# Hybrid recurrent decoder step: where the pre-sums of the last pairs are made in the down projection, when its forms are asked for, and where two loads and fillers stand in the mixer

## The chip, the cores and the metric

The kernel runs on 1 core of a Trainium2 chip. The metric is the time of one launch on the device, in microseconds (us). In the profile PE is TensorE (matmul), PEld its weight loads, DVE is VectorE, ACT is ScalarE, POOL is GpSimd, and SP is SyncE, whose queue issues all DMA transfers here.

## The reference, cut to what matters

One layer over 1024 prompt tokens and 8 x 4 sample tokens (1056 columns), D = 1024, FF = 2816, all in float32:

```
x = x + 0.5 * swiglu(rmsnorm(x, g1), w1_gu, w1_down)
x = x + Mix(rmsnorm(x, gm))            # mLSTM | retention | RG-LRU heads, then @ w_out
x = x + 0.5 * swiglu(rmsnorm(x, g2), w2_gu, w2_down)
y = rmsnorm(x, gf)

swiglu(x, w_gu, w_down):  gate, up = split(x @ w_gu);  (silu(gate) * up) @ w_down
```

Beside y the kernel returns the new recurrent states of both token sets.

## The kernel before, in words

Data lie transposed: a tile xT[k] holds 128 channels of all 1056 tokens. Every float32 operand is split into a high and a low float32r part, and every product takes three matmuls (low x high, high x low, high x high) of 264 columns in the two feed-forward parts.

**Feed-forward.** Each of the two feed-forward parts has a stage `gate_up` (gate and up projections) and a stage `down7` (down projection), and both use a seven-product scheme for 2 x 2 blocks: seven block products in place of eight, of sums and differences of blocks ("forms"). `gate_up` (line 474) runs over the 22 tiles j of FF. For each j, `gu` does its matmuls and stores the tile h(j) to DRAM (`hd`, lines 471 and 472). When both tiles of a pair p = j // 2 are there, `h_forms(p)` (line 490) is written behind the next j: it loads the two tiles back (`hr`, line 495), makes four sums on DVE (`ta`, `tb`), splits seven forms into high and low on ACT and DVE, and stores each form to DRAM (`hf`, line 507): 2 loads, 11 DVE operations, 7 ACT operations and 7 stores a pair. The pairs 0 to 7 of the ten (NP7 = 10, LATE7 = 2) are treated so. Pairs 8 and 9 wait for `down7`.

`down7` (line 545) takes the pairs in five groups of two; below they are the first to the fifth group, `gi` = 0 to 4. In each group it runs over four blocks of output channels (`mp` = 0 to 3), each with weights of its own (`down_weights`, line 522: one load of `wr`, sums on DVE, splits on ACT and DVE into `wh` and `wl`) and seven products of 12 matmuls, whose results DVE adds into xT (`add`, line 560). The 14 forms of a group stay on chip for its four blocks. After block 0 of a group the forms of the next group are asked for (line 588: 13 of them there, the fourteenth after the group, line 594). In the first group the order was another one: `h_forms(8)` after block 0, `h_forms(9)` after block 1, and the next group's forms after block 2.

**Slots.** All these wide tiles (xT, forms, hr, ta, tb) come from one pool, `blk`, of 35 slots. In `gate_up` 28 of them hold the forms of the normalised x, half of which are last read by the last j with both halves (19), the other half by j = 21. In `down7` 8 hold xT, 14 the forms of the group at work, and 13 are left for the next group's forms or for `h_forms`.

**Order of the work.** A scheduler orders each engine's instructions when the program is built, by their place in the program and by priority; the order is then fixed, and each engine runs its own list in order and waits at each instruction for what it needs. `tc.high_priority(n)` moves instructions up by n places: 100 for the loads of forms, 200 for weights, 300 for the additions that free PSUM.

**Mixer.** Near its end the mLSTM loop (`mlstm_loop`, line 1043) runs nine chunks of tokens with small matmuls and long chains on DVE, ACT and POOL. Between the chunks `fill(n)` (line 1518) puts n pieces of the output projection `w_out_main` (line 1505), 18 matmuls of 264 columns each, two pieces a unit m. xT was parked in DRAM before; its tiles 0 to 3 come back ahead of the loop, and tile m of 4 to 7 is asked for at unit m (line 1508). After the loop three pieces stand ahead of `norm` (line 1171), which normalises the heads in three column chunks c: scalings on ACT and DVE, then transposes on PE.

Of the kernel before, what the change touches and what calls it, by code (L numbers as in the profile page):

```python
# [24 lines left out]
KT = D // P  # L25
# [9 lines left out]
AHEAD = 100  # L35
AHEAD_GU = 200
AHEAD_EV = 300
LATE7 = 2
NP7 = 10
# [49 lines left out]
def build(ctx, tc, I, O, cdP, cd4):  # L89
# [19 lines left out]
    def B(name, dt=F32):  # L109
        return blk.tile([P, PITCH], dt, name=name, tag="b")[:, :BW]  # L110
# [79 lines left out]
    def split(h, l, x):  # L190
        act.copy(h, x)  # L191
        tt(l, x, h, SUB)
# [183 lines left out]
    def gu_weights(wgu, j):  # L376
        with tc.high_priority(AHEAD_GU):
            g = raw([wgu[:, j * P:(j + 1) * P]], KT, P)
            u = raw([wgu[:, FF + j * P:FF + (j + 1) * P]], KT, P)
            s12, s34 = wtile("wr", KT, P, F32), wtile("wr", KT, P, F32)  # L380
            lo, hi = slice(0, 4), slice(4, 8)
            tt(s12[:, lo], u[:, lo], u[:, hi], ADD)
            tt(s34[:, lo], g[:, lo], u[:, lo], ADD)
            tt(s12[:, hi], s12[:, lo], g[:, lo], ADD)
            tt(s34[:, hi], s12[:, hi], g[:, hi], ADD)
            hg, lg = parts(g)
            h12, l12 = parts(s12)
            h34, l34 = parts(s34)
            hu, lu = parts(u[:, hi])
        return [(hg[:, lo], lg[:, lo]), (hg[:, hi], lg[:, hi]), (h12[:, hi], l12[:, hi]), (h12[:, lo], l12[:, lo]),  # L390
                (h34[:, lo], l34[:, lo]), (h34[:, hi], l34[:, hi]), (hu, lu)]
# [82 lines left out]
    def gate_up(F, wgu, hd, hf, early, late, more):  # L474

        todo = [(j, [0, 1]) for j in range(FF // P) if j not in early + late]
        for i, j in enumerate(early):
            todo.insert(2 * i + 2, (j, [1]))
        todo += [(j, [1]) for j in late]
        ready, pend = set(), None  # L480
        for n, (j, ss) in enumerate(todo):
            gu(j, gu_weights(wgu, j), F, ss, hd, lambda: next(more, None))
            if pend is not None:
                h_forms(pend, hd, hf)
            ready.add(j)
            pend = j // 2 if j ^ 1 in ready and j // 2 < NP7 - LATE7 else None
        if pend is not None:
            h_forms(pend, hd, hf)

    def h_forms(p, hd, hf):  # L490

        v = lambda t: t.rearrange("p (s e n) -> p s e n", s=2, e=2)
        r = [B("hr") for _ in range(2)]
        for i in range(2):
            sp.dma_start(r[i], hd[(2 * p + i) * P:(2 * p + i + 1) * P, :])
        b11, b12, b21, b22 = (v(r[i])[:, :, e] for i in range(2) for e in range(2))
        w = lambda t: t.rearrange("p (i s n) -> p i s n", i=2, s=2)
        ta, tb = w(B("ta")), w(B("tb"))
        t1, t2, t3, t4 = ta[:, 0], ta[:, 1], tb[:, 0], tb[:, 1]
        tt(t1, b11, b12, SUB)  # L500
        stt(t2, t1, -1.0, b22, MUL, SUB)
        tt(t3, b22, b12, SUB)
        stt(t4, t2, -1.0, b21, MUL, SUB)
        for i, x in enumerate((b11, b21, t2, t1, t3, b22, t4)):
            f = B("hf", F32R)
            split(w(f)[:, 0], w(f)[:, 1], x)
            sp.dma_start(hf[p, i], f.bitcast(F32))
# [3 lines left out]
    ORDER = [0, 3, 2, 1, 4, 5, 6]  # L511

    def load_forms(ps_, hf, ii=ORDER):
        fs = [{} for _ in ps_]
        for i in ii:
            for d, p in zip(fs, ps_):
                f = B("hf", F32R)
                sp.dma_start(f.bitcast(F32), hf[p, i])
                d[i] = f.rearrange("p (i s n) -> p i s n", i=2, s=2)
        return fs  # L520
# [24 lines left out]
    def down7(xT, hd, hf, wd, first):  # L545
        groups = [(2 * i, 2 * i + 1) for i in range(NP7 // 2)]
        F = first

        def product(i, t, W, start):
            h, l = W[i]  # L550
            for s in range(2):
                o = t[:, s, :Q]
                for n, f in enumerate(F):
                    xh, xl = f[i][:, 0, s], f[i][:, 1, s]
                    st, sk = start and n == 0, not start
                    pe.matmul(o, l[:, n], xh, start=st, stop=False, skip_group_check=sk)  # L556
                    pe.matmul(o, h[:, n], xl, start=False, stop=False, skip_group_check=sk)  # L557
                    pe.matmul(o, h[:, n], xh, start=False, stop=n == len(F) - 1, skip_group_check=sk)  # L558

        def add(x, t, op=ADD):  # L560
            with tc.high_priority(AHEAD_EV):
                tt(x, x, t[:, :, :Q], op)

        for gi, g in enumerate(groups):
            nxt = []
            for mp in range(4):
                W = down_weights(wd, g, mp)
                x = [xT[2 * mp + i].rearrange("p (s e n) -> p s e n", s=2, e=2)[:, :, e] for i in range(2) for e in range(2)]
                x11, x12, x21, x22 = x
                b, c, a = (ps2(n) for n in ("db", "dc", "da"))  # L570
                product(0, b, W, True)
                with tc.high_priority(AHEAD_EV):
                    act.copy(a[:, :, :Q], b[:, :, :Q])
                product(3, c, W, True)
                add(x22, c, SUB)
                product(2, b, W, False)
                add(x12, b)
                product(1, a, W, False)
                add(x11, a)
                product(4, b, W, False)  # L580
                add(x22, b, SUB)
                product(5, c, W, False)
                add(x12, c)
                product(6, b, W, False)
                add(x21, b, SUB)
                if gi == 0 and mp < LATE7:
                    h_forms(NP7 - LATE7 + mp, hd, hf)
                if mp == (LATE7 if gi == 0 else 0) and gi + 1 < len(groups):
                    with tc.high_priority(AHEAD):
                        nxt = load_forms(groups[gi + 1], hf, ORDER[:6])  # L590
                        nxt[0].update(load_forms(groups[gi + 1][:1], hf, ORDER[6:])[0])
            if nxt:
                with tc.high_priority(AHEAD_GU):
                    nxt[1].update(load_forms(groups[gi + 1][1:], hf, ORDER[6:])[0])
            F = nxt
# [108 lines left out]
    def reload(ks=range(KT)):  # L704
        for k in ks:
            xT[k] = B(f"xT{k}")
            sp.dma_start(xT[k], spill[k * P:(k + 1) * P])
# [335 lines left out]
    def mlstm_loop(kT, qT, vtile, stile, ng, fc, ad, fill):  # L1043
# [127 lines left out]
        def norm():  # L1171
            mv2 = mv.rearrange("p (a c) -> p a c", c=2)
            rstd(rd, mv2[:, :, 1])
            stt(nmr, mv2[:, :, 0], -1.0, rd, MUL, MUL)
            for i in range(2):
                Y[i] = (B("yh", F32R), B("yl", F32R))
            for c, (c0, n) in enumerate(CH):
                for t in range(3 * c, 3 * c + 3):
                    for h in range(4):
                        hs = stile(t)[:, h * MD:(h + 1) * MD]  # L1180
                        a = 4 * t + h
                        if h % 2:
                            act.activation(hs, hs, AF.Identity, scale=rd[:, a:a + 1], bias=nmr[:, a:a + 1])
                        else:
                            tsc(hs, hs, rd[:, a:a + 1], MUL, nmr[:, a:a + 1], ADD)
                for i in range(2):
                    po = ps()
                    for j, o in tiles(c):
                        tr(po[:, o:o + P], stile(3 * c + j)[:, i * P:(i + 1) * P])
                    yh, yl = Y[i][0][:, c0:c0 + n], Y[i][1][:, c0:c0 + n]  # L1190
                    g = col("g_mlstm_norm", i)
                    act.mul(yh, po[:, :n], g)
                    stt(yl, po[:, :n], g, yh.bitcast(F32), MUL, SUB)
# [23 lines left out]
            if j == P8 + 1:  # L1217
                sample_update()
        statistics(NT - 1)
        fill(3)  # L1220
        norm()
        last_states()

# [281 lines left out]
    def w_out_main():  # L1505
        for s in range(2):
            for m in range(KT):
                if m > 3 and s == 0:
                    reload([m])
                u = unit([w_out[2 * P:, m * P:(m + 1) * P]], 6, P)  # L1510
                for q in (2 * s, 2 * s + 1):
                    w_out_part(ps("mm", "po"), u, 0, range(2, KT), 2, m, q)
                    yield
# [4 lines left out]
    def fill(n):  # L1518
        for _ in range(n):
            next(main, None)  # L1520
# [144 lines left out]
```

## Time and profile before

| | us |
|---|---|
| time, median of 3 runs | 2026.94 |
| the three runs | 2024.17, 2026.94, 2028.95 |
| the profiled execution, its own time | 2037.62 |
| its span, first to last instruction | 2035.8 |
| PE busy in the span | 1971.3 (97%) |
| DVE, ACT, POOL busy | 1379.8 (68%), 755.1 (37%), 128.0 (6%) |
| DMA moved | 347.03 MB, 170 GB/s on average |
| granted TensorE clock, mean | 0.982 |

The profile is of one execution, which took 10.68 us more than the median of the runs. A busy PE isn't PE at full speed: the granted clock stands beside it, as a share of full speed, and at half clock a matmul is busy for longer.

### The profile page before, as it was taken

To read this page: it belongs to the slowest core of one execution; us is meant where nothing else is said; L and a number is where in the kernel's file an instruction comes from. 1 tells how busy PE (TensorE), PEld (TensorE's weight loads), DVE (VectorE), ACT (ScalarE), POOL (GpSimd) and SP (SyncE) were. 2 spreads that over 40 slices of the span, in tenths; PEclk is the share of its full clock that TensorE was granted. 3 is DMA by queue.
4 is the path that set the end of the run, shared out by engine and by line. 5 is a ranking of instruction groups with operands and counts; after the bars stand their busy time and mean duration, and the time that the engine had idled before them with its cause. 6 is when DMAs were issued, how large, how long until landed. Compare 5 with 4: busy or idle time off the path is not lost.

```text
span 2035.8 us, 36906 instructions
## 1 busy us (share of the span) xinstructions
PE 1971.3 (97%) x15110; PEld 1932.2 (95%) x15110; DVE 1379.8 (68%) x2575; ACT 755.1 (37%) x1294; POOL 128.0 (6%) x175
## 2 busy tenths in 40 slices
PE   7999999999889999999999999999999999989998
PEld 7999999999889999999999989999999999978997
DVE  6857766647767775556668468976755664766777
ACT  6435444424222362211241324544434443422234
POOL 0000000000000033222111040000000000000000
PEclk9999999999989999999999989999999999989999
DMA  7236775667885432211111442425655566788522
GB/s 258 94 100 213 275 253 181 206 237 261 319 346 202 148 117 74 64 53 39 52 29 45 106 117 62 160 67 206 230 206 180 181 218 234 268 313 329 207 85 86
DMA packets 270927, 347.03 MB, mean 170 GB/s; under 512 B 17015, under 2 KB 219014, under 8 KB 270758
## 3 DMA queue, kind: packets, MB, share of 16 engines
q1 hardware_dynamic: 270758, 344.67, 49.1%
q8 instruction: 119, 1.95, 0.4%
q14 instruction: 50, 0.41, 0.1%
HBM read 224.82 MB, written 119.80 MB: 169 GB/s over the span
## 4 chain that ended last, share of the span: by engine, by line
PE 73%; issue 13%; DVE 7%; DMA 4%; ACT 2%; POOL 0%; SPq 0%; DVEq 0%; ACTq 0%; POOLq 0%
PE pb L430 8%; PE pb L431 7%; PE pb L432 7%; PE pj L199 4%; PE pj L200 4%; PE pj L201 4%; PE pc L431 4%; PE pc L430 4%; PE pc L432 4%; PE pa L431 2%; PE pa L430 2%; PE db L556 2%; PE pa L432 2%; PE db L557 2%; PE db L558 2%
## 5 line engine op out<-in xcount | busy, mean ns | idle before, releaser
L123 DVE TENSOR_TENSOR wl<-wr,wh 128x1024 fp32r<-128x1024 f32 (+3 forms) x442 | 362.4, 841 | 196.9 <-ACT wh L186 187.3
L186 ACT CAST wh<-wr 128x1024 fp32r<-128x1024 f32 (+2 forms) x242 | 230.0, 951 | 443.9 <-PE pj L201 146.1
L430 PE MATMUL pb<-fh,wl 128*128 128x264 f32 x1312 | 375.9, 287 | 5.3 <-DVE z L126 1.9
L431 PE MATMUL pb<-fl,wh 128*128 128x264 f32 x1312 | 373.0, 285 | 0.0
L432 PE MATMUL pb<-fh,wh 128*128 128x264 f32 x1312 | 370.4, 283 | 0.0
L430 PEld LDWEIGHTS pb<-fh,wl 128*128 128x128 f32 x1312 | 247.0, 188 | 10.2 <-DVE u L123 2.5
L431 PEld LDWEIGHTS pb<-fl,wh 128*128 128x128 f32 x1312 | 247.3, 188 | 0.0
L432 PEld LDWEIGHTS pb<-fh,wh 128*128 128x128 f32 x1312 | 247.1, 188 | 0.0
L556 PE MATMUL db<-hf,wl 128*128 128x264 f32 x640 | 187.4, 293 | 24.1 <-DVE wl L123 10.1
L123 DVE TENSOR_TENSOR wr<-wr 128x512 f32<-128x512 f32 (+1 forms) x336 | 176.1, 558 | 18.0 <-DMA wr<-in_w_ffn_gu 12.0
L199 PE MATMUL pj<-xh,wl 128*128 128x384 f32 (+1 forms) x576 | 187.8, 326 | 0.0
L201 PE MATMUL pj<-xh,wh 128*128 128x384 f32 (+1 forms) x576 | 187.0, 325 | 0.0
L557 PE MATMUL db<-hf,wh 128*128 128x264 f32 x640 | 185.8, 290 | 0.0
L200 PE MATMUL pj<-xl,wh 128*128 128x384 f32 (+1 forms) x576 | 185.8, 323 | 0.0
L558 PE MATMUL db<-hf,wh 128*128 128x264 f32 x640 | 184.9, 289 | 0.0
L430 PE MATMUL pc<-fh,wl 128*128 128x264 f32 x640 | 181.9, 284 | 0.0
L431 PE MATMUL pc<-fl,wh 128*128 128x264 f32 x640 | 181.8, 284 | 0.0
L432 PE MATMUL pc<-fh,wh 128*128 128x264 f32 x640 | 180.5, 282 | 0.0
L191 ACT CAST wh<-wr 128x256 fp32r<-128x256 f32 (+1 forms) x200 | 87.3, 490 | 246.8 <-PE dc L558 132.8
L556 PEld LDWEIGHTS db<-hf,wl 128*128 128x128 f32 x640 | 124.5, 195 | 27.6 <-issue 11.0
L558 PEld LDWEIGHTS db<-hf,wh 128*128 128x128 f32 x640 | 124.6, 195 | 0.0
L557 PEld LDWEIGHTS db<-hf,wh 128*128 128x128 f32 x640 | 124.3, 194 | 0.0
(460 smaller groups left out, 4766.5 us busy)
## 6 DMA issues: line engine op xcount, KB each, us to landing
hf<-hf SPq DMA_DIRECT2D x280, 528.0 KB
wr<-in_w_ffn_gu SPq DMA_DIRECT2D x104, 512.0 KB
hr<-hd SPq DMA_DIRECT2D x44, 528.0 KB
wr<-in_w_ffn_down SPq DMA_DIRECT2D x44, 512.0 KB
spill<-xT SPq DMA_DIRECT2D x24, 528.0 KB
xT<-spill SPq DMA_DIRECT2D x24, 528.0 KB
wr<-in_w_in SPq DMA_DIRECT2D x24, 512.0 KB
hd<-u SPq DMA_DIRECT2D x36, 264.0 KB
```

The lines of the kernel that those rows point to most:

```text
L123: tt = lambda o, a, b, op, e=dve: e.tensor_tensor(out=o, in0=a, in1=b, op=op)
L186: pin(act.copy(h, r))
L191: act.copy(h, x)
L199: pe.matmul(p, l[:, ku, m0:m0 + P], xh[:, c0:c0 + n], start=i == 0, stop=False)
L200: pe.matmul(p, h[:, ku, m0:m0 + P], xl[:, c0:c0 + n], start=False, stop=False)
L201: pe.matmul(p, h[:, ku, m0:m0 + P], xh[:, c0:c0 + n], start=False, stop=i == last)
L430: pe.matmul(o, l[:, k], xh[:, k], start=first and k == 0, stop=False, skip_group_check=not first)
L431: pe.matmul(o, h[:, k], xl[:, k], start=False, stop=False, skip_group_check=not first)
L432: pe.matmul(o, h[:, k], xh[:, k], start=False, stop=k == 3, skip_group_check=not first)
L556: pe.matmul(o, l[:, n], xh, start=st, stop=False, skip_group_check=sk)
L557: pe.matmul(o, h[:, n], xl, start=False, stop=False, skip_group_check=sk)
L558: pe.matmul(o, h[:, n], xh, start=False, stop=n == len(F) - 1, skip_group_check=sk)
```

## The change

Four edits. In `gate_up` the pre-sums of pair 8 are made as those of pairs 0 to 7; only pair 9 is left for `down7`. In `down7` the next group's forms are asked for after block 0 in every group, the first one too, and no pre-sums stand in the first group. Those of pair 9 stand in the third group (`gi == LATE7`), in the middle of the request for the fourth group's forms. In `w_out_main` tile m + 2 of xT is asked for at unit m. Of the three fillers ahead of `norm` one stays and two move behind the scalings of its first column chunk.

```diff
--- before.py
+++ after.py
@@ -483,7 +483,7 @@
             if pend is not None:
                 h_forms(pend, hd, hf)
             ready.add(j)
-            pend = j // 2 if j ^ 1 in ready and j // 2 < NP7 - LATE7 else None
+            pend = j // 2 if j ^ 1 in ready and j // 2 < NP7 - 1 else None
         if pend is not None:
             h_forms(pend, hd, hf)
 
@@ -583,11 +583,14 @@
                 add(x12, c)
                 product(6, b, W, False)
                 add(x21, b, SUB)
-                if gi == 0 and mp < LATE7:
-                    h_forms(NP7 - LATE7 + mp, hd, hf)
-                if mp == (LATE7 if gi == 0 else 0) and gi + 1 < len(groups):
+                if mp == 0 and gi + 1 < len(groups):
                     with tc.high_priority(AHEAD):
-                        nxt = load_forms(groups[gi + 1], hf, ORDER[:6])
+                        nxt = load_forms(groups[gi + 1], hf, ORDER[:3])
+                    if gi == LATE7:
+                        h_forms(NP7 - 1, hd, hf)
+                    with tc.high_priority(AHEAD):
+                        for d, e in zip(nxt, load_forms(groups[gi + 1], hf, ORDER[3:6])):
+                            d.update(e)
                         nxt[0].update(load_forms(groups[gi + 1][:1], hf, ORDER[6:])[0])
             if nxt:
                 with tc.high_priority(AHEAD_GU):
@@ -1183,6 +1186,8 @@
                             act.activation(hs, hs, AF.Identity, scale=rd[:, a:a + 1], bias=nmr[:, a:a + 1])
                         else:
                             tsc(hs, hs, rd[:, a:a + 1], MUL, nmr[:, a:a + 1], ADD)
+                if c == 0:
+                    fill(2)
                 for i in range(2):
                     po = ps()
                     for j, o in tiles(c):
@@ -1217,7 +1222,7 @@
             if j == P8 + 1:
                 sample_update()
         statistics(NT - 1)
-        fill(3)
+        fill(1)
         norm()
         last_states()
 
@@ -1505,8 +1510,8 @@
     def w_out_main():
         for s in range(2):
             for m in range(KT):
-                if m > 3 and s == 0:
-                    reload([m])
+                if s == 0 and 4 <= m + 2 < KT:
+                    reload([m + 2])
                 u = unit([w_out[2 * P:, m * P:(m + 1) * P]], 6, P)
                 for q in (2 * s, 2 * s + 1):
                     w_out_part(ps("mm", "po"), u, 0, range(2, KT), 2, m, q)
```

## Rows read from the trace of the kernel before

**Rows 1.** The page's first part: busy time, share and instructions of each engine.

```profile
PE 1971.3 (97%) x15110; PEld 1932.2 (95%) x15110; DVE 1379.8 (68%) x2575; ACT 755.1 (37%) x1294; POOL 128.0 (6%) x175
```

**Rows 2.** Stretches: groups one to three of both down stages; busy, clock, DMA, GB/s.

```profile
487.62:533.42 45.80, 44.52 (x363) 43.88 (x361) 44.81 (x96) 20.41 (x44) 0.00 (x0) 1.00 0.59 212
533.42:593.88 60.46, 49.84 (x336) 48.19 (x337) 35.11 (x74) 10.97 (x24) 0.00 (x0) 0.86 0.94 362
593.88:634.88 41.00, 41.00 (x338) 40.81 (x337) 31.34 (x64) 11.01 (x24) 0.00 (x0) 1.00 0.62 238
1758.90:1802.97 44.07, 44.07 (x363) 43.85 (x361) 42.76 (x83) 20.45 (x44) 0.00 (x0) 1.00 0.60 218
1802.97:1868.15 65.18, 51.10 (x338) 49.23 (x337) 34.98 (x71) 10.98 (x24) 0.00 (x0) 0.84 0.87 332
1868.15:1909.36 41.21, 41.16 (x338) 40.81 (x337) 31.42 (x64) 11.01 (x24) 0.00 (x0) 1.00 0.64 242
```

**Rows 3.** Waits of PE in the second group, first down stage: us, times, longest.

```profile
PE db L556 <- DVE wl L123: 5.6, 2, 3.4
PE db L556 <- DMA hf<-hf: 2.9, 2, 2.3
PE da L556 <- DMA hf<-hf: 1.8, 2, 1.2
```

**Rows 4.** Timeline of SP's queue, end of the first group and second: start, length, instruction.

```profile
527.38 0.32 SPq L507 DMA_DIRECT2D hf<-hf  x1
527.79 0.38 SPq L518 DMA_DIRECT2D hf<-hf  x1
...
549.83 0.38 SPq L180 DMA_DIRECT2D wr<-in_w_ffn_down  x1
551.12 16.88 SPq L518 DMA_DIRECT2D hf<-hf  x13
569.03 0.38 SPq L180 DMA_DIRECT2D wr<-in_w_ffn_down  x1
```

**Rows 5.** Waits of SP's own queue, 480 to 700 us: us in total, times, longest.

```profile
SPq L507 <- DVE hf L123: 28.2, 9, 11.8
```

**Rows 6.** Stretches around the start of the first down stage; columns as in Rows 2.

```profile
428.00:452.00 24.00, 24.00 (x200) 24.00 (x199) 13.08 (x20) 7.22 (x11) 0.00 (x0) 1.00 0.31 100
452.00:487.60 35.60, 35.56 (x287) 34.74 (x286) 18.19 (x28) 14.52 (x26) 0.00 (x0) 1.00 0.90 325
495.00:532.00 37.00, 37.00 (x306) 36.92 (x305) 36.76 (x78) 15.82 (x35) 0.00 (x0) 1.00 0.60 215
550.00:575.00 25.00, 22.70 (x169) 22.26 (x170) 12.13 (x22) 2.82 (x6) 0.00 (x0) 0.93 1.03 417
```

**Rows 7.** Timeline of SP's queue at the end of the first `gate_up`.

```profile
411.77 2.71 SPq L518 DMA_DIRECT2D hf<-hf  x4
...
451.68 5.20 SPq L518 DMA_DIRECT2D hf<-hf  x5
...
476.31 0.38 SPq L180 DMA_DIRECT2D wr<-in_w_ffn_down  x1
```

**Rows 8.** Instructions on the tile hf, 495 to 536 us: ns min/median/max, first, last.

```profile
L123 DVE TENSOR_TENSOR hf<-hr,hf x6: 696/699/700, 504.3 to 534.0; 128x528 fp32r<-128x528 f32 x6
```

**Rows 9.** The page's DMA issues: count and size of one.

```profile
hf<-hf SPq DMA_DIRECT2D x280, 528.0 KB
...
wr<-in_w_ffn_down SPq DMA_DIRECT2D x44, 512.0 KB
```

**Rows 10.** Timeline of DVE in the mixer, with the idle time before and its releaser.

```profile
1204.67 0.77 DVE L123 TENSOR_TENSOR xT<-po,xT 128x264 f32<-128x264 f32 x2 [2.46 <-DMA xT<-spill]
```

**Rows 11.** Timeline of PE in the mixer at the same place.

```profile
1206.24 0.96 PE L1113 MATMUL ps<-va,wk 128*128 128x65 f32 x7 [2.24 <-DVE cs L123]
```

**Rows 12.** Stretches in the mixer; columns as in Rows 2.

```profile
1208.00:1212.00 4.00, 4.00 (x24) 3.78 (x24) 3.67 (x19) 0.00 (x0) 0.70 (x2) 0.57 0.67 195
1242.00:1253.00 11.00, 9.04 (x42) 7.62 (x41) 8.27 (x28) 8.34 (x22) 0.00 (x0) 0.69 0.25 73
```

## The prediction

> **What bounds the kernel now.** I start with the page's engine totals: PE is busy for 1971.3 of 2035.8 us [rows 1], so time can be won only where PE waits or runs at a lower clock. Windows over the whole span show where: almost all of it lies in the two down stages and a little in the mixer. So the next view is one window a group of a down stage [rows 2]. The third group is what a well-fed group looks like: 41.00 us in the first stage, 41.21 in the second, PE busy throughout, clock 1.00. The second group does the same work in 60.46 and 65.18 us. Its excess is 19.46 + 23.97 = 43.4 us. In the first stage 60.46 - 49.84 = 10.6 us of that is idle time of PE; the rest, 8.8 us, is the granted clock, 0.86 on average, since it fell to its lower level (1.2 in place of 2.4 GHz) behind these pauses. The first groups, 45.80 and 44.07 us, lose 4.8 and 2.9.
>
> PE's waits say for what the second group waited: 4.7 us for forms (2.9 + 1.8) and 5.6 us for split weights [rows 3]. SP's queue says why. The first load of the second group's forms goes out at 527.79, right behind a store of pair 9's forms at 527.38 [rows 4], with the group due at 533.4. That store had waited for DVE: SP stood 28.2 us in nine such waits, the longest 11.8 us [rows 5]. DVE was busy for 36.76 of the 37 us before, because the sums of two pairs lie in the first group [rows 6]. Later, 13 loads for the third group (551.12 to 568.0) stand between two weight loads, at 549.83 and 569.03 [rows 4], while DMA is saturated at 417 GB/s [rows 6]. So the stall is a queue: late DVE, a blocked store, loads behind it, weights behind these.
>
> **The change part by part.**
>
> *Pre-sums out of the first group, forms asked for at once.* A pair costs 11 DVE operations of 0.70 us [rows 8], 7.7 us. Two pairs off the first group bring DVE from 44.81 to 29.4 us, near the third group's 31.34 [rows 2]. Thirteen slots are free when the stage starts (35 less 8 of xT and 14 forms), so 13 forms of 0.541 MB (528 KB, [rows 9]) can go at once: 7.0 MB, 16.9 us at 417 GB/s, due some 41 us later. That is the case of the third group. I take both second groups at 1 us over a third one: 43.4 - 2 = 41.4 us gained. Bounds: nothing gained, and all 43.4 with the first groups' 7.7 on top (51.1).
>
> *Pair 8 in `gate_up`.* Its 7.7 us of DVE lie beside PE: between 428 and 452 us DVE is busy for 13.08 of 24 us and PE for all 24 [rows 6]. Its 2 loads and 7 stores, 9 x 0.541 = 4.9 MB or 11.7 us, find DMA busy for 0.31 of these 24 us [rows 6], so 16 us are free. But it holds the spare slots. The four forms loaded at 411.77 [rows 7], and three tiles of xT just behind, come only when pair 8's stores are done, two j later, about 452. The stretch from 452 to 487.6 then carries 325 GB/s x 35.6 us = 11.6 MB and 7 x 0.541 = 3.8 MB more: 15.4 MB, 36.8 us at 417 GB/s, 1.2 us more than there is. With that, the first weight load of the stage (476.31, [rows 7]) lands later too. I take 2 us a stage, +4. Bounds: 0 (four of these tiles are needed only in blocks 2 and 3), and what the rate already seen in that stretch gives: 15.4 MB at 325 GB/s is 47.3 us, 11.7 late, +23.4 in both stages.
>
> *Pair 9 in the third group.* DVE would have 31.34 + 7.7 = 39.0 of 41 us. DMA would have 14 forms, 2 loads, 7 stores and 4 weights of 0.524 MB: 14.5 MB, 34.9 us. Both fit. I read the priorities so: all 13 loads (100 places up, the sums being 27 instructions) get slots before the sums do, so these run as the third group's forms are released in its block 3, at the border to the fourth. Their results are needed a whole group later. Queued behind a store that waits for DVE are the fourteenth form of the fourth group, due 6/7 of a block or 8.8 us into it, weights, and the fifth group's loads. I take 1.5 us a stage, +3. Bounds: 0, and the stall of the second group, +43.4 in both.
>
> The Trainium skill speaks against these two parts: "DMA: Bandwidth & Descriptors", section Specifications, gives one core's share of HBM as about 358 GB/s. By that, estimated, the 15.4 MB take 42.9 us, 7.3 late, and the third group's 14.5 MB take 40.5 of its 41 us: the sum would be 10.6 us longer. The row shows 417 GB/s over 25 us of loads and stores [rows 6], so I keep the row.
>
> *x two units ahead.* DVE stood 2.46 us for a tile of xT [rows 10], PE then 2.24 us for DVE [rows 11], and from 1208 to 1212 the clock was 0.57 [rows 12], 1.7 us more. With the request two units earlier that goes, 3.9 us; I take 3, because an earlier request can stand before transfers of the chunks. Bounds: -3.9, and +3.9 for the same pause at another chunk.
>
> *Fills split.* Between 1242 and 1253 PE loses 1.96 us idle and 0.31 x 11 = 3.4 us of clock [rows 12]. `norm` has no PE instruction before the transposes of its first chunk, so all three pieces still run ahead of them and end when they did: 0. Bounds: -5.4, and +4.4 if the two pieces (36 matmuls of 41.00/336 = 0.122 us) end behind the transposes.
>
> **Sum.** -41.4 + 4 + 3 - 3 + 0 = -37.4 us of 2037.62 for the profiled execution: 2000.2. The median of the runs lies 10.68 us below that execution. If those 10.68 us are spread over what stays, the runs go to 2026.94 - 37.4 = 1989.5; if they lie in the very stalls that go, to 2026.94 - 26.7 = 2000.2. I take the middle, 1995.
>
> **The rivals.**
>
> *A. Weights behind the forms.* The 13 loads asked for at once stand before weight loads of the first group, whose lead is short (476.31 for a start at 487.6). The second group shows the price: 5.6 of its 10.3 us of listed waits were for weights, so 0.54 of 19.46 and 23.97, 23.6 us, less the 2 that I left there: 2017. Against it: the third group has the same 13 loads and no wait.
>
> *B. Late start.* The last stretch of `gate_up` moves data no faster than it does now: 11.7 us late a stage in place of 2, +19.4: 2014. For it: that stretch is 0.90 full already, with hand-offs of slots in it. Against it: at 417 GB/s it nearly fits.
>
> *C. The stall moves, and the kernel gets slower.* Pair 9's stores stand in SP's queue between loads, at the border of third and fourth group, and wait for DVE as they did at that of first and second. It decides from about 8.8 us of wait on: then the fourteenth form is late, PE pauses, the clock falls, and weights and the fifth group's loads pile up as before. Priced as the second groups were, 43.4 less my 3: +40.4, 2035. For it: 39.0 of 41 us of DVE, and a longest wait of 11.8 us in the same pattern. Against it: one pair, not two; and what queues behind is, but for one form and weights, due a group later.
>
> *D. It doesn't do what it says.* No slots come free for the first group's request, and the second group stays as it is: 2026.94 + 4 + 3 - 3 = 2031.
>
> *E. The lower DMA rate.* Loads mixed with stores run at a lower rate than in the 25 us of the row, so that the stretch before the stage ends 7.3 us late: +10.6, 2006. For it: only 362 GB/s over the whole second group [rows 2]; against it, that group has waits in it. By the page's 358 GB/s, this is what would come.
>
> **How the numbers follow.** Forecast 0.55, A 0.12, B 0.15, C 0.09, D 0.04, E 0.03, and 0.02 for more than I sum up. The forecast's own range is 1985 to 2004. The range, 1981 to 2021, takes in A, B and E and most of the bounds below; C and D and the far tails stay outside. A measurement of this kernel can tell about 0.2%, 4 us. Faster by more than that: all but C and D and a little of A and B, 0.84; within it: 0.06; slower: 0.10 (C, and part of D).
>
> **What would show it.** Right: second groups of 41 to 43 us at clock 1.00, no wait of PE for hf there; loads of forms in SP's queue before 500 us; no store of line 507 in the first group. Pair 8's term: the time from the last product of `gate_up` to the first of the stage, and the length of the first group's block 0. Pair 9's: third and fourth groups of 41 to 43 us and SP's waits for DVE at line 507 under some 9 us. x: no wait of DVE for xT. Fills: the same pause ahead of the transposes. Wrong: a fourth group of 60 us (C), a first group well over 46 us with waits for wl (A), or one that starts 10 us late (B).

## The result, and the profile after

The changed kernel takes 1994.46 us (median of four runs, 1990.73 to 1995.68); beside it the kernel before took 2026.49 (2024.17 to 2028.95). The ratio is 0.9839, 95% interval 0.9821 to 0.9856: 32.0 us faster, and 0.5 us from the forecast of 1995. The profiled execution took 1990.73 us, its span 1988.9, at a mean clock of 0.996. It lies 3.7 us below its median, that of before lay 10.7 above; so the two spans differ by 46.9 us and the medians by 32.0.

The engine totals of after, beside [rows 1]: PE is busy 23.4 us less, with the same 15110 matmuls, because fewer of them ran at half clock.

```profile
PE 1947.9 (98%) x15110; PEld 1912.6 (96%) x15110; DVE 1378.4 (69%) x2575; ACT 755.8 (38%) x1294; POOL 128.1 (6%) x175
```

Windows of after over the groups one to four of both down stages, with the columns of [rows 2]:

```profile
486.40:539.07 52.67, 46.86 (x363) 46.14 (x362) 37.10 (x86) 12.91 (x30) 0.00 (x0) 0.94 0.81 305
539.07:579.97 40.90, 40.90 (x339) 40.75 (x338) 31.41 (x64) 11.01 (x24) 0.00 (x0) 1.00 0.62 235
579.97:621.15 41.18, 40.95 (x338) 40.74 (x337) 33.68 (x62) 13.77 (x28) 0.00 (x0) 1.00 0.76 277
621.15:661.91 40.76, 40.76 (x338) 40.76 (x337) 31.50 (x65) 12.87 (x28) 0.00 (x0) 1.00 0.74 282
1731.63:1781.68 50.05, 46.09 (x363) 45.37 (x361) 35.10 (x72) 13.10 (x30) 0.00 (x0) 0.97 0.82 310
1781.68:1822.56 40.88, 40.88 (x338) 40.74 (x337) 31.39 (x64) 11.00 (x24) 0.00 (x0) 1.00 0.64 243
1822.56:1863.49 40.93, 40.93 (x338) 40.77 (x337) 33.59 (x62) 13.66 (x28) 0.00 (x0) 1.00 0.77 278
1863.49:1904.55 41.06, 41.06 (x338) 40.81 (x337) 31.48 (x65) 12.16 (x27) 0.00 (x0) 1.00 0.77 289
```

The second groups are now like the others: 40.90 and 40.88 us at full clock, from 60.46 and 65.18 [rows 2]. The first groups have become the long ones: 52.67 and 50.05, from 45.80 and 44.07. Two of the columns say how: PE is idle for 5.8 us of the first of them (52.67 - 46.86), and its clock is 0.94.

Waits of PE in groups one to three of the first stage of after (us, times, longest), beside [rows 3]. No wait for `hf` is left; both waits for split weights lie in the first group, 1.73 us at its block 1 and 4.08 at its block 3:

```profile
PE db L556 <- DVE wl L123: 5.8, 2, 4.1
```

Where the split weights were late, in the timelines of PE, ACT and DVE of after (start, length, instruction, in brackets the idle time before and its releaser):

```profile
526.51 0.56 PE L556 MATMUL db<-hf,wl 128*128 128x264 f32 x1 [4.08 <-DVE wl L123]
```

```profile
517.55 1.02 ACT L191 CAST wh<-wr 128x256 fp32r<-128x256 f32 x3 [3.22 <-DMA wr<-in_w_ffn_down]
526.06 2.21 ACT L191 CAST wh<-wr 128x512 fp32r<-128x512 f32 x5 [7.49 <-DVE wr L123]
```

```profile
515.20 0.70 DVE L123 TENSOR_TENSOR xT<-xT,dc 128x528 f32<-128x528 f32 x1 [2.20 <-PE dc L558]
...
522.46 0.70 DVE L123 TENSOR_TENSOR xT<-xT,db 128x528 f32<-128x528 f32 x1 [0.75 <-PE db L558]
523.09 0.16 DVE L124 TENSOR_SCALAR spw<-spl 128x2 f32<-128x2 f32 x1
...
524.94 1.09 DVE L123 TENSOR_TENSOR wr<-wr 128x256 f32<-128x256 f32 x3
```

The weights of the first group's block 3 landed just before 517.55, when ACT began to cast them. Their sums on DVE (`wr<-wr`) began only at 524.94. In between DVE was not short of time: it stood before each addition into xT and waited for PE. Its list simply has block 2's last four additions and ten tiny operations ahead of the sums. PE ran out of split weights and stood for 4.08 us; in the later part of that wait and behind it the clock was at its lower level (1.2 GHz), in the window here at 0.50:

```profile
524.80:531.60 6.80, 5.09 (x23) 5.12 (x24) 6.69 (x19) 3.79 (x8) 0.00 (x0) 0.50 0.42 137
```

SP's queue of after around the first group, beside [rows 4, 7]. The forms for the second group now go out from 491.21 on, not from 527.79. The load of block 3's weights stands behind all thirteen of them, at 509.04 (before: 494.47):

```profile
491.21 0.32 SPq L518 DMA_DIRECT2D hf<-hf  x1
492.07 0.38 SPq L180 DMA_DIRECT2D wr<-in_w_ffn_down  x1
493.28 12.22 SPq L518 DMA_DIRECT2D hf<-hf  x12
...
509.04 0.38 SPq L180 DMA_DIRECT2D wr<-in_w_ffn_down  x1
```

And in the third group, with pair 9's loads (L495) and stores (L507) between the forms (L518):

```profile
571.07 4.69 SPq L518 DMA_DIRECT2D hf<-hf  x7
580.46 0.38 SPq L180 DMA_DIRECT2D wr<-in_w_ffn_down  x1
580.93 0.93 SPq L495 DMA_DIRECT2D hr<-hd  x2
...
596.43 3.46 SPq L507 DMA_DIRECT2D hf<-hf  x4
603.49 0.32 SPq L518 DMA_DIRECT2D hf<-hf  x1
604.06 0.32 SPq L507 DMA_DIRECT2D hf<-hf  x1
604.79 8.26 SPq L518 DMA_DIRECT2D hf<-hf  x6
613.10 2.05 SPq L507 DMA_DIRECT2D hf<-hf  x2
```

Pair 9's stores go out from 596.43 to 615, inside the third group (579.97 to 621.15), not at its border.

### The profile page after: what moved, and what is told of

The parts are those of the page before. It is cut to its first block, busy times and chain, and to the rows that moved or that the text cites. A ratio compares the mean times of both kernels' runs of the same rounds, so it can differ in the third digit from the quotient of the medians.

```text
span 1988.9 us, 36911 instructions
## 1 busy us (share of the span) xinstructions
PE 1947.9 (98%) x15110; PEld 1912.6 (96%) x15110; DVE 1378.4 (69%) x2575; ACT 755.8 (38%) x1294; POOL 128.1 (6%) x175
## 4 chain that ended last, share of the span: by engine, by line
PE 88%; DVE 6%; ACT 2%; DMA 2%; issue 1%; POOL 1%; DVEq 0%; SPq 0%; POOLq 0%; ACTq 0%
PE pb L430 8%; PE pb L431 8%; PE pb L432 8%; PE pj L199 4%; PE pj L201 4%; PE pj L200 4%; PE pc L430 4%; PE pc L431 4%; PE pc L432 4%; PE db L556 4%; PE db L557 4%; PE db L558 3%; PE dc L557 2%; PE dc L556 2%; PE dc L558 2%; PE pa L430 2%
## 5 line engine op out<-in xcount | busy, mean ns | idle before, releaser
L556 PE MATMUL db<-hf,wl 128*128 128x264 f32 x640 | 183.4, 287 | 10.3 <-DVE wl L123 9.8
L557 PE MATMUL db<-hf,wh 128*128 128x264 f32 x640 | 182.9, 286 | 0.0
L558 PE MATMUL db<-hf,wh 128*128 128x264 f32 x640 | 181.9, 284 | 0.0
L556 PEld LDWEIGHTS db<-hf,wl 128*128 128x128 f32 x640 | 121.5, 190 | 12.2 <-issue 10.5
L558 PEld LDWEIGHTS db<-hf,wh 128*128 128x128 f32 x640 | 121.4, 190 | 0.0
L557 PEld LDWEIGHTS db<-hf,wh 128*128 128x128 f32 x640 | 121.1, 189 | 0.0
```

## Experiments

The theory: the gain comes from the second groups, and needs both the early request and the sums out of the first group; the first groups pay for the request. The rivals: the request alone does it; the sums' places don't matter; the mixer's edits carry part of it. "The changed kernel" below is after, and group lengths are from first product to first product in one profiled execution.

**The request of the first group one block later.**

```diff
-                if mp == 0 and gi + 1 < len(groups):
+                if mp == (1 if gi == 0 else 0) and gi + 1 < len(groups):
```

> The changed kernel, but in the first group the next group's forms are asked for after its second block instead of its first. Theory (weights behind the forms): in the changed kernel the first groups take 52.7 and 50.1 us because 12 forms stand in SP's queue ahead of the weights of blocks 2 and 3; asked later, the first groups come back to 44 to 47 us, the second stay at 41, and the time is about 1994.5 - 11 = 1983. Rival (crowded transfers since 440 us and a fixed DVE order are to blame, not this request): first groups stay near 50 us and the time at 1992 to 1997.

1989.97 us against 2026.85 of before, ratio 0.9814 (0.9795 to 0.9833). First groups 46.21 and 46.22, second 40.73, but fourth groups 42.66 and 42.65. Most of what the first groups pay in the changed kernel is thus due to when the forms are asked for. One block later is still early enough for the second groups. The time is 7 us above the expected 1983; 3.5 of these lie in the fourth groups, which the expectation had left out.

**In two parts: six forms after block 0, seven after block 1.**

```diff
                     if gi == LATE7:
                         h_forms(NP7 - 1, hd, hf)
+                if mp == (1 if gi == 0 else 0) and gi + 1 < len(groups):
                     with tc.high_priority(AHEAD):
                         for d, e in zip(nxt, load_forms(groups[gi + 1], hf, ORDER[3:6])):
```

> The changed kernel, but in the first group only the first six forms of the next group are asked for after block 0, the other seven after block 1. Theory (each form ahead of the weights costs): six forms hold the weights half as long as twelve, so the first groups lie between 46.2 (all asked later) and 52.7 and 50.1 (all at once), about 47 to 49 us; time 1988 to 1993. Rival (the loss steps in where the twelve stand ahead of one certain load of weights): first groups 46 us as with all asked later, 1984 to 1990.

1988.98 us against 2027.16, ratio 0.9812 (0.9797 to 0.9827): the lowest median here, though the interval still touches the changed kernel's. First groups 46.19 and 46.03 (10.5 us less than there in sum), second 40.69, fourth 42.65 and 42.66 (3.5 more). The first groups are at the rival's 46, not at 47 to 49: the loss does not grow form by form, and the six forms cost nothing. Windows of its first and fourth group, and the timelines of DVE, ACT and SP's queue at block 3's weights:

```profile
489.04:535.22 46.18, 44.45 (x362) 43.82 (x361) 33.73 (x79) 13.04 (x30) 0.00 (x0) 1.00 0.87 336
...
616.64:659.29 42.65, 41.09 (x338) 40.82 (x337) 31.50 (x63) 13.30 (x28) 0.00 (x0) 1.00 0.81 310
```

```profile
517.22 1.09 DVE L123 TENSOR_TENSOR wr<-wr 128x256 f32<-128x256 f32 x3
```

```profile
516.39 0.58 ACT L573 COPY da<-db 128x528 f32<-128x528 f32 x1 [7.61 <-PE db L558]
516.88 1.02 ACT L191 CAST wh<-wr 128x256 fp32r<-128x256 f32 x3
```

```profile
505.04 0.38 SPq L180 DMA_DIRECT2D wr<-in_w_ffn_down  x1
505.51 4.75 SPq L518 DMA_DIRECT2D hf<-hf  x7
```

Block 3's weights go out ahead of the seven later forms, and the trace has their last piece landed at 510.97, 21.9 us after the group's first product; in the changed kernel it is 517.47, 31.1 us after it. ACT casts them only at 516.88, because its list has a copy that waits for PE ahead of the cast. DVE's sums stand ahead of block 2's additions here and begin at 517.22, and block 3 starts at 525.05 without a wait. So both moved, the transfer and the place of the sums, and this run can't tell one from the other. The changed kernel's own trace says more: its weights landed at 517.47, PE needed them at 522.43, and from the start of the sums to block 3's first product it took 1.6 us (524.94 to 526.51). By that estimate sums begun on landing would have been in time. So the late transfer alone need not have stopped PE, and the list was the last link; that is argued from one trace, not shown by a run.

**The request alone: before, with the first group's forms asked for after block 0 and both pairs' sums behind it, in the first group.**

```diff
-                if gi == 0 and mp < LATE7:
-                    h_forms(NP7 - LATE7 + mp, hd, hf)
-                if mp == (LATE7 if gi == 0 else 0) and gi + 1 < len(groups):
+                if mp == 0 and gi + 1 < len(groups):
...
+                if gi == 0 and mp < LATE7:
+                    h_forms(NP7 - LATE7 + mp, hd, hf)
```

> The kernel before, but the first group's request is made after its first block, ahead of the sums of pairs 8 and 9, which both stay in the first group. Theory (the order of the request is what mattered): the second group falls to 41 to 44 us; the third group's forms now stand behind pair 9's stores, so that one may take 45 to 50 us; time 1995 to 2010. Rival (DVE full with two pairs in the first group is what mattered): first or second group stay long, 2020 to 2030.

2019.74 us, ratio 0.996 (0.9945 to 0.9976). Second groups 52.49 and 52.70, first 48.92 and 47.14, third 44.40 and 43.38. That is on the rival's side (2020 to 2030), outside the theory's range: asking at once gains 7 us of the 32; without the sums moved out, some 11.5 us of the second group's excess stay in each stage. The other half alone, both sums moved out and the request left behind block 2, was not run. So it is shown that the request alone does not do it, but not that the second groups need it as early as this. Waits of PE in its second group, and of SP at L507 there (`issue` is time for which the profile shows no releaser, so what held PE in the longest wait stays open):

```profile
PE db L556 <- issue: 6.0, 1, 6.0
PE db L556 <- DVE xT L123: 3.2, 1, 3.2
```

```profile
SPq L507 <- DVE hf L123: 14.4, 9, 8.8
```

**Pair 8's sums in the first group, in the middle of its request; pair 9's as in the changed kernel.**

```diff
-            pend = j // 2 if j ^ 1 in ready and j // 2 < NP7 - 1 else None
+            pend = j // 2 if j ^ 1 in ready and j // 2 < NP7 - LATE7 else None
...
-                    if gi == LATE7:
-                        h_forms(NP7 - 1, hd, hf)
+                    if gi in (0, LATE7):
+                        h_forms(NP7 - (1 if gi else 2), hd, hf)
```

> The changed kernel, but the sums of pair 8 stand in the first group again, in the middle of its request, as those of pair 9 stand in the third group's. Theory (the second group's stall came from the order of SP's queue: request behind two pairs' stores): six forms go out first, seven behind pair 8's stores, so the second group waits a little for its later forms, 43 to 47 us, while the first is near 46: 1990 to 1998. Rival (the stall came from a full DVE alone): with one pair DVE has 37 of 45 us, second group 41 us, start of the stage earlier: about 1985. Rival (pair 8 has to be out of the first group): second groups 50 us or more, 2010 to 2020.

1998.24 us, ratio 0.9856 (0.9841 to 0.987), 3.8 us above the changed kernel's median. First groups 44.12, second 46.33, fourth 44.61, each in both stages: what the first groups get back (14.5 us in sum), the second and fourth ones lose and more (10.9 and 7.4). Pair 8 in `gate_up` is the better place by these sums, though the intervals of the two ratios overlap.

**Pair 9's sums behind the whole request of the third group.**

```diff
-                    if gi == LATE7:
-                        h_forms(NP7 - 1, hd, hf)
                     with tc.high_priority(AHEAD):
...
+                    if gi == LATE7:
+                        h_forms(NP7 - 1, hd, hf)
```

> The changed kernel, but the third group's request is not split: all 13 forms first, then pair 9's sums, which then run at the border to the fourth group. Theory (what queues behind them is due a whole group later): fourth and fifth groups 41 to 43 us, time 1993 to 1999. Rival C of the prediction (the stall moves to this border): fourth groups 50 to 65 us, time 2015 to 2035.

2009.38 us, ratio 0.9907 (0.989 to 0.9923), 14.9 above the changed kernel. Third groups 42.44 and 42.27, fourth 46.68 and 46.56. Its fourth group, SP's wait at L507 in it, and SP's queue at the border (625.83):

```profile
625.83:672.51 46.68, 42.53 (x339) 42.35 (x337) 34.31 (x65) 13.64 (x30) 0.00 (x0) 0.96 0.86 324
```

```profile
SPq L507 <- DVE hf L123: 12.0, 5, 10.5
```

```profile
615.23 0.81 SPq L495 DMA_DIRECT2D hr<-hd  x2
626.60 6.63 SPq L507 DMA_DIRECT2D hf<-hf  x7
633.33 13.90 SPq L518 DMA_DIRECT2D hf<-hf  x14
```

This has the pattern of rival C: sums at the border, stores that wait 10.5 us for DVE, loads behind them. It costs about 7 us a stage in the two groups, not 20, and not through the fourteenth form: PE waited for no form in that fourth group, but 4.2 us for split weights.

**Four more places for pair 9 or the request**, all on the kernel with the request in two parts (1988.98 us). Pair 9 in the second group:

```diff
-                    if gi == LATE7:
+                    if gi == 1:
```

> As the kernel that asks in halves in the first group (1988.98 us), but pair 9's sums in the second group in place of the third. If the 42.65 us of the fourth group there come from pair 9's stores standing between the loads of that group's forms, the cost moves with the sums: the third group then takes 42 to 43 us, the fourth about 40.8, and the time is the same, 1987 to 1992. If the fourth group is long for a reason of its own, it keeps its 42.6 and the third stays at 40.7.

2002.71 us, ratio 0.9877 (0.9859 to 0.9895). Third groups 47.24 and 48.38, fourth 41.17 and 40.90: the cost moved with the sums, and grew. Pair 9 ahead of the whole request:

```diff
+                if mp == 0 and gi == LATE7:
+                    h_forms(NP7 - 1, hd, hf)
                 if mp == 0 and gi + 1 < len(groups):
```

> As the kernel that asks in halves in the first group (1988.98 us), but pair 9's sums are written ahead of the whole request for the fourth group's forms, not in its middle. In SP's order the stores then stand three, three and one between the loads (there: four, then three behind seven loads). If it is the last store in front of the last loads that makes the fourth group late, its four loads behind six stores still wait: fourth groups of 42 to 45 us, 1988 to 1994. If an earlier start of the sums is enough, fourth groups of about 40.8 and 1984 to 1986.

1993.87 us, ratio 0.9836 (0.9815 to 0.9858). Third groups 44.01 and 44.46, fourth 43.58 and 42.36: an earlier start is no help (the stores go out from 582.02 on, 8.3 us into the third group, there from 593.99, 18.1 us into it). The third group's last block is now the long one (13.49 and 13.94 us, in place of 10.17). Ten forms after block 0 and three after block 1:

```diff
+                    K = 5 if gi == 0 else 3
...
-                        nxt = load_forms(groups[gi + 1], hf, ORDER[:3])
+                        nxt = load_forms(groups[gi + 1], hf, ORDER[:K])
```

> The changed kernel, but in the first group ten forms are asked for after block 0 and three after block 1 (six and seven gave 1988.98 us). SP's order in the third group is then nearly that of the changed kernel: four stores, a form, a store, six forms, two stores, a form. If that order is what spares the fourth group (40.76 us there, 42.65 with four stores, seven forms, three stores), fourth groups of about 40.8 us. If first groups pay for each form that stands before the weight loads of block 2 and 3, they lie between 46.2 and 52.7 us, about 48 to 50. Sum: 1986 to 1993 us.

1993.41 us against 2031.23, ratio 0.9811 (0.9776 to 0.9845). The time is just above its range. First groups 47.84 and 47.67, between the others, a little under the expected 48 to 50: six forms ahead cost nothing, ten 1.6 us a group, thirteen 4 to 6.5. Its two stages have different queues in the third group. In the first the stores stand as in the changed kernel (four, one and two among the forms), and its fourth group takes 40.69; in the second, as below, it takes 42.65:

```profile
1842.46 6.49 SPq L507 DMA_DIRECT2D hf<-hf  x4
1851.06 7.22 SPq L518 DMA_DIRECT2D hf<-hf  x7
1858.32 1.37 SPq L507 DMA_DIRECT2D hf<-hf  x3
```

So the 2 us of the fourth group go with the order in which pair 9's stores and the forms stand. Pair 9 behind eleven forms in place of seven (`K = 3 if gi == 0 else 5`):

> First group asked in halves as in the kernel of 1988.98 us; in the third group eleven of the fourteen forms for the fourth group are asked for before pair 9's sums and three behind. If what costs is the number of forms that stand behind pair 9's stores, fewer do (three behind two and five stores, in place of seven behind four), and fourth groups take about 40.8 us: 1984 to 1987 us. If it is the time at which the sums get their slots, they run later, nearer to the border of third and fourth group, as in the kernel with the sums behind the whole request: third and fourth groups of 42.4 and 46.6, 1995 to 2001 us.

1993.14 us, ratio 0.9812 (0.9772 to 0.9853). Fourth groups 44.78 and 46.96: fewer forms stand behind the stores, but those go out only from 609.01 on. That speaks for the later start, in part: the third groups stay at 40.77 and 40.76, where 42.4 was expected, and the time lies between the two ranges.

**The mixer's edits.** The changed kernel without them (`reload([m])` and `fill(3)` as before):

> The changed kernel without its two mixer edits (x asked for at its own unit again, three fillers ahead of norm). Theory (the mixer's edits give about 4 us: the 2.2 us pause for xT and its clock): 1994.5 + 4 = 1998, ratio 0.986. Rival (they give what one profiled execution shows between first mlstm matmul and the transposes of norm, 9.5 us): 2004, ratio 0.989. Rival (that stretch is 74 to 82 us in one and the same code by the granted clock, and the edits give nothing): 1994 to 1996, ratio 0.984.

1993.34 us, ratio 0.9832 (0.9816 to 0.9848): nothing that can be told from the whole change. Before with the x edit alone:

```diff
-                if m > 3 and s == 0:
-                    reload([m])
+                if s == 0 and 4 <= m + 2 < KT:
+                    reload([m + 2])
```

> The kernel before with x asked for two units ahead and nothing else. Theory (the pause of DVE for a tile of xT goes and no other takes its place): no DVE wait for xT behind its reload, 2 to 4 us less, ratio 0.998 to 0.999. Rival (the pause is hidden anyway or comes back at another chunk): ratio 1.000 within its interval, with a new wait of PE of 1 to 3 us in the loop.

2026.43 us against 2027.16, ratio 1.0003 (0.999 to 1.0016). DVE's wait for xT is still there, 2.13 us long, and PE waits 2.27 us at 1204.99 behind it. DVE's row and SP's queue in this kernel:

```profile
1203.54 0.43 DVE L123 TENSOR_TENSOR xT<-po,xT 128x264 f32<-128x264 f32 x1 [2.13 <-DMA xT<-spill]
```

```profile
1172.96 1.36 SPq L707 DMA_DIRECT2D xT<-spill  x1
1174.43 22.30 SPq L1059 DMA_DIRECT2D wk<-ad  x3
1197.11 0.33 SPq L707 DMA_DIRECT2D xT<-spill  x1
```

The second tile was written two units earlier, yet it went out at 1197.11, where before it went at 1198.67: in SP's list it stands behind three loads of `wk` (L1059), the last of which left 22.3 us after the first. Before with the fills split alone (`fill(1)` ahead of `norm`, `fill(2)` in its first chunk):

> The kernel before with the fillers split and nothing else. Forecast of the prediction: 0, PE's order the same, ratio 1.000. Rival (the pause of 1.6 us ahead of the transposes of norm goes, as the changed kernel's PE waits have none there): 1 to 3 us less, ratio 0.9985 to 0.9995.

2028.03 us, ratio 0.9999 (0.9985 to 1.0012): nothing, as priced.

## Why the prediction was right, step by step

Per step, in the profiled executions of before and after (the length of `gate_up` is from its first product to the stage's first):

| step | predicted | measured |
|---|---|---|
| second groups | -41.4 | -43.9 (-19.6, -24.3) |
| first groups | 0 (rival A: +23.6) | +12.9 (+6.9, +6.0), of these +3.2 in block 0 |
| pair 8, length of `gate_up` | +4 (with block 0) | -3.0 (-1.9, -1.1) |
| pair 9, third and fourth groups | +3 | +0.3 |
| fifth groups | not named | -3.3 (-2.0, -1.3) |
| x and fills | -3 and 0 | ratios 1.0003 and 0.9999, each alone |

The rows measured in these two profiles sum to -37.0 us. The spans differ by 46.9: another 10.6 lie in the mixer, from the end of the first down stage to `gate_up`'s first product (622.98 and 612.42 us). In the other kernels that stretch took 612.1 to 619.0 us, the same code 612.1 in one execution and 623.0 in the other, so this is no effect of the change.

**Second groups: right**, in cause and size. They take as long as third groups now, with no wait for forms. Given the early request, moving the sums was worth 25.3 us between the medians (2019.74 and 1994.46).

**First groups: the step that failed.** I wrote of the thirteen forms asked for at once "That is the case of the third group" and gave the first group nothing but its gain. In the third group DMA is busy for 0.62 of the time [rows 2]; the first group begins behind a stretch at 0.90 [rows 6], and its last weight load stands behind the request. Rival A had the place and the wait (for `wl`), at about twice the price: without block 0, which is pair 8's, the request cost 9.7 us, and nothing where it was made in two parts. What rival A had not was the end of the chain: by the estimate above the weights landed in time, and their sums stood too far back in DVE's list.

**Pair 8: about the price, in block 0.** The prediction named two places to look. The length of `gate_up` tells nothing: with pair 8 in it, the first one took 397.7 to 400.3 us in nine kernels, without it 399.1 to 399.7 in five (the second: 416.1 to 417.7, and 416.3 to 417.4), so -3.0 lies within what single executions differ by. The first group's block 0 tells more: with pair 8 in `gate_up` it took 15.4 us in every stage, without it 13.4 to 14.5, on average 13.8. That is 1.6 us a stage, 3.2 in both, near the 4 predicted. It comes by late weights, as predicted, only by block 1's and not by the first ones: their load went out at 486.93 (before: 482.49), and PE waited 1.73 us for them, where it had no such wait before. Windows of after, beside the first two of [rows 6]:

```profile
428.00:452.00 24.00, 24.00 (x200) 24.00 (x199) 18.99 (x29) 11.13 (x18) 0.00 (x0) 1.00 0.68 238
452.00:486.40 34.40, 34.35 (x278) 33.53 (x276) 17.80 (x28) 14.04 (x25) 0.00 (x0) 1.00 0.96 353
```

The work of pair 8 went where I had put it, 138 GB/s more ahead of 452, and less came after 452 than I had counted: 353 x 34.4 = 12.1 MB, not 15.4. I had kept the 417 GB/s of [rows 6] against rival E as a rate "of loads and stores". It is a rate of loads: no store leaves SP's queue between 550 and 575, and no stretch read here shows the rate of loads mixed with many stores.

**Pair 9: small, but for another reason.** I read the priorities so that its sums would run at the border. They ran inside the third group, between the parts of the request, and the stores waited for DVE only 4.4 us at the longest. With the sums at the border the kernel takes 2009.38: the place that I had assumed would have cost 14.9 us, not 3.

**x: no gain.** The pause stayed, 2.03 us in the changed kernel; the request had moved in the code, and the second tile in SP's list hardly. In the profiled executions the loop took 75.7 to 82.3 us in the ten kernels with the x edit, and 72.9, 73.1, 73.7 and 82.0 in the four without it (from its first matmul to the last product with the carried state): nothing here speaks for a gain.

**From profile to median.** I took the middle between two readings of the 10.7 us by which the profiled execution lay above the median. The one with the fills alone, 2027.88 us, shows what they were: its second groups are 4.0 us shorter in sum (61.61 and 60.09), its mLSTM loop 9.1 us (72.90, against 82.00 before). Less than half of the 10.7 lay in the stalls that go.

So the main term was right in cause and size, and that the sum came within 0.5 us of 1995 was luck. In these profiles the steps sum to -37.0, where -37.4 was predicted: the first groups' +12.9 and the 3 us that x did not give were offset by 7.0 for pair 8 (the spread of `gate_up` in it), 2.7 for pair 9, 2.5 in the second groups and 3.3 in the fifth ones.

**Left open.** Why DVE's list puts the sums so late, and what that alone costs, was not tried by a change of the list alone. The sums moved out with the request where it was before were not run. What shortens the fifth groups wasn't isolated. Nor was the pause ahead of `norm`'s transposes: with the x edit, the way from the loop's last product with the carried state to the first transpose is 12.31 us (13.07 to 13.10 without), also where the fills are as before.

## What to carry to other kernels

An early request is paid by what stands behind it in the same queue: count what is already in flight at that place, not only the bytes of the request, and hand it over in parts. Then look for the last step in the lists of the other engines: data that has landed is of no use while an engine with a fixed order stands at another instruction. An engine's start on data doesn't tell when the data landed: it may have stood at something else. For a moved line of code, look where its transfer really leaves the queue. And before a stage's difference between two profiles is called an effect, look how far executions with the same code for that stage differ.

## What the runs showed of the hardware

The rate of DMA in the crowded first group, in slices of 1.1 us from 486 to 530 us of after:

```profile
GB/s 392 342 363 417 397 417 392 385 419 394 400 427 414 403 419 415 430 419 419 422 419 415 426 422 404 383 377 369 130 23 0 7 0 0 0 0 0 0 65 351
```

While the queue is full it is 342 to 430 GB/s, most of it above 380; that is near the 417 of [rows 6], and again of loads with few stores. From 452 to 486.40 the mean is 353 at a DMA share of 0.96, though there, too, SP's queue sends out 24 loads and only two stores, of 264 KB each. What lowers it is not shown; no transfer was issued from 454.3 to 459.2 and from 467.9 to 475.0. The Trainium skill, "DMA: Bandwidth & Descriptors", section Specifications, gives about 358 GB/s a core as the limit of HBM. The crowded loads exceed that, and the stretch before them comes near it; the late start of the stage that the prediction worked out from it did not come.

The mLSTM loop, the same code in the kernel before and in the one with the request alone, took 82.00 us in one execution and 73.74 in the other. A difference of that size between two profiles there tells no effect.
